# One decoder step: the keys' rotation in larger operations, a transpose without its copy, a split made one block ahead, and a new order in layer 1

## The chip, the cores and the metric

The kernel runs on one core of a Trainium2 chip. The metric is device time in microseconds of one execution; lower is better. The engines go by short names: PE (TensorE, matmuls and transposes; PEld is its weight load), DVE (VectorE), ACT (ScalarE), POOL (GpSimd), SP (SyncE, which issues most DMAs).

## The reference, cut to what matters

One step of a two-layer decoder on 512 prompt tokens and 8 x 4 sample tokens (544 columns), model width 1024. Layer 0 mixes tokens with a gated linear recurrence (HGRN2), layer 1 with sparse attention: an indexer scores all keys, the best are kept, and softmax attention runs over those. In both layers the tokens also attend to 256 memory tokens, and each layer ends with a gated channel mixer. What the change touches in layer 1:

```python
def dsa_project(z, pos, q_norm, k_norm, ik_norm):
    q, k, v, iq, ik, iw = jnp.split(z, np.cumsum(DSA_SIZES)[:-1].tolist(), axis=-1)
    q = rope(rms_norm(q.reshape(B, T, N_Q_HEADS, HEAD_DIM), q_norm), pos)      # 6 heads of 128
    k = rope(rms_norm(k.reshape(B, T, N_KV_HEADS, HEAD_DIM), k_norm), pos)     # 2 heads of 128
    iq = rope(iq.reshape(B, T, IDX_HEADS, IDX_DIM), pos)                       # 8 heads of 64
    ik = rope(rms_norm(ik, ik_norm)[:, :, None, :], pos)[:, :, 0, :]           # 1 head of 64
def rope(x, pos):     # x1, x2: the halves of the last axis
    return jnp.concatenate([x1 * cos - x2 * sin, x2 * cos + x1 * sin], axis=-1)
def memory_keys_values(mem, w_kv, k_norm):
    k, v = jnp.split(mem @ w_kv, 2, axis=-1)
    return rms_norm(k.reshape(B, M, MEM_HEADS, MEM_HD), k_norm), v.reshape(B, M, MEM_HEADS, MEM_HD)
def memory_attention(zq, q_norm, mk, mv):
    q = rms_norm(zq.reshape(B, T, MEM_HEADS, MEM_HD), q_norm)
    s = jnp.einsum('bthd,bmhd->bhtm', q, mk) * (MEM_HD ** -0.5)
```

## The kernel before

All products are of fp32 quality: both factors are split into a high part and a low rest, and three matmuls, high x high, high x low and low x high, are summed in PSUM. The weights come as 199 units of 128 x 1024 in the order in which they are used (class `Weights`). Each is loaded (`raw`), copied by ACT to `whi`, and DVE or POOL subtracts to get `wlo`; in layer 1 POOL does it in four pieces of 256 columns (`W.piece`), and the loads are issued from POOL's queue (`W.queue`). Activations are split into `hi` and `lo` in the same way (`split`).

Every engine works through its own list in order; the lists are fixed when the program is built. The main program walks through the projections (`proj_fm` for outputs with features on the partitions, 48 matmuls of 272 columns for one unit of weights; `proj_tm` for outputs with tokens on the partitions). All else (norms, rotations, the indexer, the choice of keys, attention) is written as Python generators that issue a few instructions and yield. Between the groups of matmuls the main program calls `pump.run`, and there the string `SCRIPT` says which generators take a step: each letter or sign names a generator in the order of their making, a number repeats, a dot ends the call. A "+" or "-" in it answers a question: is this unit's `wlo` made by DVE (+) or POOL (-), is a row scaling (`scale_rows`) done by ACT (+) or DVE (-). So `SCRIPT` alone sets what stands ahead of what on each engine.

Layer 1 runs in this order: index keys and queries (`ikT`: transposes of the rotated index keys `ikr`; `id`: scores of the prompt's queries, which use `ikm`, a masked copy of `ikT`), v, the six query heads q with the first memory loads in between, k, attention, memory queries (mq) and memory keys and values (mkv). Beside the query heads run the steps of `choose_sample`, which searches the threshold of the best keys of the sample tokens by counting: each step is a few short DVE operations, three counts on DVE and four on ACT, and a small matmul (`ple_choose_sample` in the trace) that joins the counts. `choose_prompt` does the same for prompt tokens with MAX8 and MATCH_REPLACE8 on DVE; these have time and act as fillers. `query_scale` computes the norm factors of all query heads (`qss`, `rq`, `rqs`) and transposes those of the sample tokens (`qrb`).

`key_rope` rotates keys for index keys (5 tiles of 128 tokens, 1 head of 64) and for keys (2 + 2 + 1 tiles, 2 heads of 128): POOL multiplies by the cosine (into `ikr` or `kr`), DVE the swapped halves by the sine (`t_index_keys`, `t_keys`), then DVE subtracts and adds. `mem_kv` projects the memory: four blocks of `raw` memory columns, each split into high and low and then multiplied with one weight unit (matmul `mkv` of 512 columns). `mem_samples` computes the norm factors of the sample tokens' memory queries (`m_mem_samples`, `mrs`), spreads four of them over 64 columns each with a POOL copy (`rqx`), and transposes that into PSUM (`mb`) to scale the queries (`mqz`).

## Time and profile before

| | us |
|---|---|
| median of 3 timed runs | 1492.82 (1492.29 to 1493.84) |
| the profiled execution's own time | 1481.36 |
| its span in the trace | 1479.6 |
| mean granted clock of PE | 0.982 of 2.4 GHz |
| PE busy | 1428.4 |
| DVE, ACT, POOL busy | 797.0, 587.3, 578.5 |

The profiled execution was one of its own, beside the timed runs; its time is the span and 1.8 us around it. All durations below are from it. "Busy" counts an engine's instructions without its waits.

### The profile page before, as it was taken

Reading aid. Unit: us, or ns where it says so; the run is one execution under the profiler, and the core shown is the slowest. Engines: PE = TensorE matmul, PEld = TensorE weight load, DVE = VectorE, ACT = ScalarE, POOL = GpSimd, SP = SyncE. Lnnn points to the kernel's source line nnn. Section 1 sums busy time; section 2 is a strip of 40 time slices with the busy share of each in tenths; the row PEclk is TensorE's granted clock in tenths of the full one; section 3 lists DMA queues with packets and bytes.
Section 4 is the critical chain, followed back from the end, with each engine's and each line's share of the span. In section 5 each row is a group of like instructions: output and inputs, shape, how many; then the busy total and the mean of one; then the engine's idle time right before and its main releaser. Section 6 shows DMA issues by size and latency. Waiting matters only on the chain.

```text
span 1479.6 us, 28277 instructions
## 1 busy us (share of the span) xinstructions
PE 1428.4 (97%) x11314; PEld 1341.1 (91%) x11314; DVE 797.0 (54%) x1762; ACT 587.3 (40%) x1064; POOL 578.5 (39%) x663
## 2 busy tenths in 40 slices
PE   7989999999999999999999987799999999999998
PEld 7968889999999999999987876466999999999998
DVE  7366877754444224444378879876544442344431
ACT  5447465533333113333326452575333331233320
POOL 4332354423444024446764554460134441144410
PEclk9999999999999999999999997999999999999999
DMA  7341223222322322334322425750223333222331
GB/s 246 129 141 62 75 91 102 89 86 77 99 88 86 100 72 86 91 92 125 123 89 66 152 94 172 238 177 28 86 77 92 93 89 88 82 86 87 92 117 58
DMA packets 58995, 152.54 MB, mean 103 GB/s; under 512 B 7888, under 2 KB 21808, under 8 KB 58864
## 3 DMA queue, kind: packets, MB, share of 16 engines
q1 hardware_dynamic: 49792, 122.84, 27.0%
q0 software_dynamic: 8208, 26.50, 5.4%
q8 instruction: 89, 1.46, 0.4%
q10 hardware_dynamic: 864, 1.40, 0.3%
q14 instruction: 42, 0.34, 0.1%
HBM read 142.23 MB, written 8.47 MB: 102 GB/s over the span
## 4 chain that ended last, share of the span: by engine, by line
PE 84%; DVE 7%; issue 3%; POOL 2%; ACT 2%; DMA 1%; SPq 0%; ACTq 0%; POOLq 0%; DVEq 0%
PE a L420 73%; PE u_hgrn_head L420 1%; POOL wlo L420 1%; PE id_index_prompt L420 1%; PE ho_hgrn_head L420 1%; PE ms_prompt L420 1%; PE hgrn_head_samples L420 1%; PE as_prompt_attn L420 1%; DVE lo L420 1%; PE mkv L420 1%; PE mo_prompt L420 1%; PE sc_hgrn_head L420 1%; DMA raw<-w 1%; PE ao_prompt_attn L420 1%; PE mpt_prompt L420 1%
## 5 line engine op out<-in xcount | busy, mean ns | idle before, releaser
L420 POOL TENSOR_TENSOR wlo<-raw,whi 128x1024 fp32r<-128x1024 f32 (+1 forms) x206 | 353.9, 1729 | 560.1 <-ACT whi L420 536.0
L420 PE MATMUL a<-hi,whi 128*128 128x272 f32 x2640 | 554.6, 291 | 0.8 <-DVE ext L420 0.5
L420 PE MATMUL a<-lo,whi 128*128 128x272 f32 x2640 | 548.9, 289 | 5.6 <-DVE lo L420 5.6
L420 PE MATMUL a<-hi,wlo 128*128 128x272 f32 x2640 | 548.0, 289 | 0.0
L420 PEld LDWEIGHTS a<-hi,whi 128*128 128x128 f32 x2640 | 416.0, 189 | 8.5 <-issue 5.6
L420 PEld LDWEIGHTS a<-lo,whi 128*128 128x128 f32 x2640 | 416.2, 189 | 7.0 <-DVE lo L420 7.0
L420 PEld LDWEIGHTS a<-hi,wlo 128*128 128x128 f32 x2640 | 416.7, 189 | 0.0
L420 ACT ACTIVATE whi<-raw 128x1024 fp32r<-128x1024 f32 (+1 forms) x202 | 209.5, 1038 | 243.9 <-PE a L420 153.6
L420 DVE TENSOR_TENSOR wlo<-raw,whi 128x1024 fp32r<-128x1024 f32 (+1 forms) x59 | 79.4, 1345 | 161.4 <-ACT whi L420 161.2
L420 DVE TENSOR_TENSOR sc<-a,rb 128x544 f32<-128x544 f32 x53 | 38.4, 725 | 114.9 <-PE a L420 113.3
L420 DVE SCALAR_TENSOR_TENSOR conv<-ext,params,conv 128x560 f32<-128x560 f32 x88 | 70.6, 802 | 47.7 <-ACT conv L420 46.2
L420 DVE TENSOR_TENSOR ext<-a,rb 128x240 f32<-128x240 f32 x132 | 37.6, 340 | 105.8 <-PE a L420 98.3
L420 ACT ACTIVATE conv<-ext,params 128x560 f32<-128x560 f32 x44 | 37.7, 856 | 135.0 <-DVE ext L420 114.1
L420 ACT ACTIVATE hi<-sc 128x544 fp32r<-128x544 f32 x44 | 29.0, 659 | 137.5 <-DVE sc L420 137.5
L420 DVE TENSOR_TENSOR x<-a,x 128x544 f32<-128x544 f32 x48 | 34.7, 723 | 78.9 <-PE a L420 78.5
L420 POOL TENSOR_TENSOR sqa<-sqa,sq 128x544 f32<-128x544 f32 x24 | 34.7, 1447 | 107.4 <-ACT sq L420 107.1
L420 DVE TENSOR_TENSOR sc<-sc,conv 128x512 f32<-128x512 f32 x88 | 65.8, 786 | 4.6
L420 ACT ACTIVATE conv<-conv 128x560 f32<-128x560 f32 x44 | 29.6, 672 | 73.8 <-DVE conv L420 73.8
L420 ACT ACTIVATE hi<-x,params 128x544 fp32r<-128x544 f32 x32 | 23.8, 745 | 68.9 <-DVE x L420 68.9
L420 DVE TENSOR_TENSOR lo<-sc,hi 128x544 fp32r<-128x544 f32 x44 | 31.9, 725 | 31.9 <-ACT hi L420 31.9
L420 PE MATMUL a<-whi,hi 128*128 128x256 f32 x160 | 47.0, 294 | 0.0
L420 PE MATMUL a<-whi,lo 128*128 128x256 f32 x160 | 45.1, 282 | 0.0
(406 smaller groups left out, 1918.0 us busy)
## 6 DMA issues: line engine op xcount, KB each, us to landing
raw<-w SPq DMA_DIRECT2D x177, 512.0 KB, 3.5
raw<-w POOLq DMA_DIRECT2D x21, 512.0 KB, 4.1
k_sample_scores<-ckT SPq DMA_DIRECT2D x46, 128.0 KB, 2.1
ck_mem_samples<-cmkT SPq DMA_DIRECT2D x16, 256.0 KB, 5.5
cv_mem_samples<-cmv SPq DMA_DIRECT2D x16, 256.0 KB, 5.6
st_s<-hgrn_head_samples POOLq DMA_DIRECT2D x12, 256.0 KB, 3.0
hgrn_head_samples<-hst SPq DMA_DIRECT2D x10, 256.0 KB, 3.8
ck_sample_scores<-ckT SPq DMA_DIRECT2D x18, 128.0 KB, 2.3
```

The lines of the kernel that those rows point to most:

```text
L420: return f(*args, **kw)
```

## The change

Four edits. `key_rope` takes its cosine and sine from views over all tiles of a key tensor (`qtab`, `itab` are now one view for each tensor), and so multiplies a whole tensor's half at once: for the index keys 2 operations of 128x160 on each of POOL and DVE instead of 10 of 128x32, for the keys 6 on each instead of 10. `mem_samples` leaves out the copy `rqx`: four matmuls with the identity take the broadcast factor itself as the other operand (32 x 64), each giving 64 of the 128 rows of `mb`. `mem_kv` splits block u + 1 before the matmuls of block u. And the part of `SCRIPT` that plays layer 1 is another one, of the same number of calls.

```diff
-    "12.+12.+17.-e6.e2.-2.e8.-5.-2f2.f5.f3.-.f9.-4.f.f9.-gh6.3g.16g2i12gi2gi4gj4gi8gh2g4hjij2h.-ijihjl.lij.i.ji.j.ij."
+    "12.+12.+17.-e6.e2.-2.e8.-5.-2f2.f3.f5.+3.f7.+4.f7.f.2g.h.+4.g.g.2g.26gi2g2hi4gigj2i7gighghjig2hjijg.-ghihjilij4."
...
@@ mem_kv
+        pump.run(raw[0])
+        x = split(raw[0][:, :512], sl=slice(0, 512), eng=G if POOLED else V)
         for u in range(4):
+            xh, xl = x
             if len(raw) < min(u + 3, 4):
                 mem_load(raw)
-            pump.run(raw[u])
-            xh, xl = split(raw[u][:, :512], sl=slice(0, 512), eng=G if POOLED else V)
             hi, lo = W.next()
+            if u < 3:
+                pump.run(raw[u + 1])
+                x = split(raw[u + 1][:, :512], sl=slice(0, 512), eng=G if POOLED else V)
@@ mem_samples
-        rx = slot(name="rqx")
-        G.tensor_copy(v3(rx[0:NS, :256], 4, 64), v3(rq[0:NS], 5, 4)[:, 4, :].unsqueeze(2).to_broadcast([NS, 4, 64]))
-
-        yield [rx]
+
+        yield [rq]
         bb = bank("mb")
         for j in range(2):
-            T.transpose(bb[:, 32 * j:32 * j + 32], rx[0:NS, 128 * j:128 * j + 128], ident[0:NS, 0:NS])
+            for e in range(2):
+                T.matmul(bb[64 * e:64 * e + 64, 32 * j:32 * j + 32],
+                         rq[0:NS, 16 + 2 * j + e:17 + 2 * j + e].to_broadcast([NS, 64]), ident[0:NS, 0:NS],
+                         start=True, stop=True, skip_group_check=True)
@@ key_rope
-            for i in range(n):
-                c4 = tabs[at][:, 0:hf].unsqueeze(1).to_broadcast([128, nh, hf])
-                s4 = tabs[at][:, hf:].unsqueeze(1).to_broadcast([128, nh, hf])
-                for sl, other in ((slice(0, hf), slice(hf, d)), (slice(hf, d), slice(0, hf))):
-                    G.tensor_mul(f(t1)[:, i, :, sl], k4[:, i, :, sl], c4)
-                    V.tensor_mul(f(t2)[:, i, :, sl], k4[:, i, :, other], s4)
-                at += 1
+            cs, sn = (tab[:, :, sl].unsqueeze(2).to_broadcast([128, n, nh, hf]) for sl in (slice(0, hf), slice(hf, d)))
+            for sl, other in ((slice(0, hf), slice(hf, d)), (slice(hf, d), slice(0, hf))):
+                G.tensor_mul(f(t1)[:, :, :, sl], k4[:, :, :, sl], cs)
+                V.tensor_mul(f(t2)[:, :, :, sl], k4[:, :, :, other], sn)
@@ layer 1
-    qtab = [tt[j // 4][:, 128 * (j % 4):128 * (j % 4) + 128] for j in range(5)]
-    itab = [tt[1][:, 128 + 64 * j:192 + 64 * j] for j in range(5)]
+    qtab = [v3(tt[0][:, 0:256], 2, 128), v3(tt[0][:, 256:512], 2, 128), v3(tt[1][:, 0:128], 1, 128)]
+    itab = [v3(tt[1][:, 128:448], 5, 64)]
```

In layer 0 the order of the instructions stays as it was but for the two edited functions. In layer 1 the new `SCRIPT` gives seven more weight units' `wlo` to DVE: two of the v projection, one of the first query head, two of the k projection and two of the output projection (59 before, 66 now); five row scalings go from DVE to ACT. Among its moves: choice step 2 of the sample tokens stands behind 42 of the 48 matmuls of the first query head, where it stood behind 12 of the next one. Three places of the new order follow; names carry a number that only tells tiles apart.

DVE at the index keys' rotation, before (`rq`, `t_2`, `t_3`: the rotation of index queries):

```order
L420 TENSOR_TENSOR ikt_index_keys_2_8490<-ikt_index_keys_2_8490,params_79 128x320
L420 TENSOR_TENSOR rq_8564<-a_8483,tab_8305 128x544
L420 TENSOR_TENSOR t_2_8565<-a_8483,tab_8307 64x544 x2
L420 TENSOR_TENSOR t_index_keys_1_8584<-ikt_index_keys_2_8490,tt_8293 128x32 x10
L420 TENSOR_TENSOR rq_8647<-a_8577,tab_8305 128x544
L420 TENSOR_TENSOR t_3_8648<-a_8577,tab_8307 64x544 x2
L420 TENSOR_TENSOR ikr_8463<-ikr_8463,t_index_keys_1_8584 128x5x32 x2
L420 TENSOR_TENSOR wm_8302<-wm_index_keys_1_8707,consts_81 128x32
```

The same place now:

```order
L420 TENSOR_TENSOR ikt_index_keys_2_8490<-ikt_index_keys_2_8490,params_79 128x320
L420 TENSOR_TENSOR rq_8564<-a_8483,tab_8305 128x544
L420 TENSOR_TENSOR t_2_8565<-a_8483,tab_8307 64x544 x2
L420 TENSOR_TENSOR wlo_8571<-raw_8316,whi_8570 128x1024
L420 TENSOR_TENSOR t_index_keys_1_8593<-ikt_index_keys_2_8490,tt_8293 128x5x32 x2
L420 TENSOR_TENSOR rq_8628<-a_8574,tab_8305 128x544
L420 TENSOR_TENSOR t_3_8629<-a_8574,tab_8307 64x544 x2
L420 TENSOR_TENSOR wlo_8635<-raw_8399,whi_8634 128x1024
L420 TENSOR_TENSOR ikr_8463<-ikr_8463,t_index_keys_1_8593 128x5x32 x2
```

The products `t_index` are now two, and a weight split stands ahead of them and another ahead of `ikr`.

PE at the transposes of the rotated index keys, before, where 18 matmuls of the last index query projection (`a_8660`) and then the v projection (`a_8780`) stand behind them:

```order
L420 MATMUL ikT_index_keys_2_8696<-consts_80,ikr_8463 64x32
L420 MATMUL wm_index_keys_1_8707<-sc_8459,consts_81 128x32
L420 MATMUL a_8660<-hi_8110,whi_8474 128x272 x2
L420 MATMUL a_8660<-lo_8111,whi_8474 128x272 x2
L420 MATMUL a_8660<-hi_8110,wlo_8475 128x272 x2
L420 MATMUL a_8660<-hi_8196,whi_8474 128x272 x2
L420 MATMUL a_8660<-lo_8197,whi_8474 128x272 x2
L420 MATMUL a_8660<-hi_8196,wlo_8475 128x272 x2
L420 MATMUL a_8660<-hi_8282,whi_8474 128x272 x2
L420 MATMUL a_8660<-lo_8283,whi_8474 128x272 x2
L420 MATMUL a_8660<-hi_8282,wlo_8475 128x272 x2
L420 MATMUL a_8780<-whi_8570,hi_7670 128x256
```

The same place now:

```order
L420 MATMUL a_8638<-lo_8283,whi_8474 128x272 x2
L420 MATMUL a_8638<-hi_8282,wlo_8475 128x272 x2
L420 MATMUL ikT_index_keys_1_8698<-consts_80,ikr_8463 64x128 x4
L420 MATMUL ikT_index_keys_2_8699<-consts_80,ikr_8463 64x32
L420 MATMUL wm_index_keys_1_8710<-sc_8459,consts_81 128x32
L420 MATMUL id_index_prompt_1_8747<-ikm_8464,rq_8468 128x256
L420 MATMUL a_8762<-whi_8570,hi_7670 128x256
```

The projection (`a_8638`) is now complete ahead of `ikT`, and the first scores `id` follow `wm` at once.

DVE at the query scale, before, where MATCH_REPLACE and MAX of `choose_prompt` stand between the copy of `qss` and its chain:

```order
L420 COPY qss<-qst_query_squares_1_9970 128x5x3
L420 MATCH_REPLACE isc_index_prompt_2_8889<-_prompt_choose_prompt_2_8940,isc_index_prompt_2_8889 128x384
L420 MATCH_REPLACE isc_index_prompt_1_8843<-_prompt_choose_prompt_2_8886,isc_index_prompt_1_8843 128x256
L420 MAX _prompt_choose_prompt_1_8939<-isc_index_prompt_2_8889 128x8
L420 TENSOR_TENSOR qss<-qss,rs_8290 128x30 x2
L420 TENSOR_SCALAR qss<-qss 128x30
L420 TENSOR_SCALAR m_query_scale_1_10013<-qss 128x30
```

The same place now:

```order
L420 COPY qss<-qst_query_squares_1_9924 128x5x3
L420 TENSOR_SCALAR _sample_choose_sample_2_9021<-_sample_choose_sample_9_9931,_sample_choose_sample_2_9021 128x7
L420 TENSOR_SCALAR _sample_choose_sample_1_9020<-_sample_choose_sample_2_9021 128x1
L420 TENSOR_TENSOR _sample_choose_sample_1_9020<-_sample_choose_sample_1_9020 128x7
L420 TENSOR_TENSOR _sample_choose_sample_1_9020<-_sample_choose_sample_1_9020 128x1
L420 TENSOR_TENSOR _sample_choose_sample_1_9020<-consts_81,_sample_choose_sample_1_9020 128x7
L420 TENSOR_SCALAR _sample_choose_sample_1_9025,_sample_choose_sample_4_9023<-row_index_sample_3_9015,_sample_choose_sample_1_9020,_sample_choose_sample_2_9021 128x264 x3
L420 TENSOR_TENSOR qss<-qss,rs_8290 128x30 x2
L420 TENSOR_SCALAR qss<-qss 128x30
L420 TENSOR_SCALAR m_query_scale_1_9979<-qss 128x30
```

The choice step of the sample tokens that stood ahead of the copy now stands behind it, and the chain follows without `choose_prompt`'s operations.

DVE at the memory block, before; eight operations on `sbias` follow, then the additions `kr`, the memory norm factors and the second `lo`:

```order
L420 COPY m_mem_samples_1_10439<-mst_mem_samples_1_10440 128x5x2
L420 TENSOR_TENSOR t_keys_1_10447<-v_10060,tt_8292 128x2x64 x4
L420 TENSOR_TENSOR t_keys_2_10448<-v_10063,tt_8292 128x2x64 x4
L420 TENSOR_TENSOR t_keys_3_10449<-v_last_1_10085,tt_8293 128x2x64 x2
L420 TENSOR_TENSOR lo_10492<-mem_8769,hi_10491 128x512
L420 COPY m_mem_samples_1_10439<-mst_mem_samples_2_10504 128x5x2
L420 COPY _sample_choose_sample_2_9044<-ample_choose_sample_13_10544 128x2
L420 SCALAR_TENSOR_TENSOR _sample_choose_sample_1_9048<-consts_80,_sample_choose_sample_2_9044,row_index_sample_3_9039 128x256
L420 SCALAR_TENSOR_TENSOR _sample_choose_sample_1_9048<-consts_80,_sample_choose_sample_2_9044,row_index_sample_3_9039 128x8
L420 SCALAR_TENSOR_TENSOR _sample_choose_sample_1_9048<-_sample_choose_sample_1_9048,row_index_sample_3_9039 128x264
L420 SCALAR_TENSOR_TENSOR _sample_choose_sample_1_9048<-row_index_sample_3_9039,_sample_choose_sample_2_9044,_sample_choose_sample_1_9048 128x264
```

The same place now:

```order
L420 TENSOR_TENSOR t_keys_1_10442<-v_10027,tt_8292 128x4x64 x2
L420 TENSOR_TENSOR t_keys_2_10443<-v_10030,tt_8292 128x4x64 x2
L420 TENSOR_TENSOR t_keys_3_10444<-v_last_1_10052,tt_8293 128x2x64 x2
L420 COPY m_mem_samples_1_10465<-mst_mem_samples_1_10467 128x5x2
L420 TENSOR_TENSOR kr_10046<-kr_10046,t_keys_1_10442 128x4x64 x2
L420 TENSOR_TENSOR kr_10047<-kr_10047,t_keys_2_10443 128x4x64 x2
L420 TENSOR_TENSOR kr_10048<-kr_10048,t_keys_3_10444 128x2x64 x2
L420 COPY m_mem_samples_1_10465<-mst_mem_samples_2_10480 128x5x2
L420 TENSOR_TENSOR lo_10489<-mem_8751,hi_10466 128x512
L420 MATCH_REPLACE isc_index_prompt_1_8812<-_prompt_choose_prompt_1_8891,isc_index_prompt_1_8812 128x256
L420 TENSOR_TENSOR m_mem_samples_1_10465<-m_mem_samples_1_10465,rs_8290 128x20 x2
```

The additions `kr` and the first `lo` now come directly behind `t_keys`, and the memory norm factors behind them.

On PE the transposes `kT` of `kr`, which stood behind the first 12 matmuls `mkv` and 8 sample scores, now stand ahead of these.

## Rows read from the trace of the kernel before

**Rows 1.** Part 1 of the page: busy time of each engine, its share of the span, and its instructions.
```profile
PE 1428.4 (97%) x11314; PEld 1341.1 (91%) x11314; DVE 797.0 (54%) x1762; ACT 587.3 (40%) x1064; POOL 578.5 (39%) x663
```

**Rows 2.** Busy time by stretches, layer 0 with the start of layer 1, and the channel mixer of layer 1. Columns: stretch in us, its length, busy us (and instructions) of each engine, granted clock of PE as a share of 2.4 GHz, busy share of the DMA engines, GB/s.
```profile
0.00:750.00 750.00, 735.86 (x5932) 703.83 (x5933) 394.21 (x799) 307.20 (x512) 307.42 (x318) 0.99 0.33 104
...
1029.00:1479.60 450.60, 446.63 (x3561) 446.01 (x3559) 172.32 (x268) 130.65 (x158) 139.48 (x145) 1.00 0.28 86
```

**Rows 3.** The same view for the rest of layer 1 (first row) and, inside it, for seven stretches of 3.4 to 10.2 us.
```profile
750.00:1029.00 279.00, 245.95 (x1825) 191.31 (x1823) 230.47 (x697) 149.43 (x394) 131.60 (x201) 0.93 0.40 128
774.90:778.30 3.40, 3.40 (x18) 3.40 (x17) 0.00 (x0) 3.25 (x11) 1.11 (x2) 0.50 0.25 82
829.50:832.90 3.40, 3.40 (x17) 3.40 (x16) 3.25 (x9) 0.70 (x3) 2.19 (x3) 0.50 0.82 274
877.30:884.10 6.80, 5.74 (x34) 4.24 (x34) 4.56 (x26) 4.15 (x13) 2.25 (x5) 0.50 0.78 260
901.20:911.40 10.20, 5.87 (x21) 4.25 (x15) 9.95 (x35) 0.90 (x2) 4.90 (x9) 0.50 0.47 142
918.30:925.10 6.80, 5.31 (x15) 3.67 (x19) 4.75 (x18) 0.50 (x1) 2.02 (x5) 0.50 0.84 247
945.60:949.00 3.40, 3.40 (x28) 1.50 (x30) 2.90 (x14) 0.76 (x3) 0.00 (x0) 0.50 0.74 247
959.20:962.60 3.40, 3.40 (x19) 1.42 (x20) 2.26 (x10) 1.36 (x5) 2.49 (x4) 0.51 0.74 239
```

**Rows 4.** PE's timeline at its waits in layer 1. Columns: start, busy us, engine, line, operation, out<-in, shape, count; in brackets the idle time before and who ended it.
```profile
773.41 0.77 PE L420 MATMUL ikT_index_keys<-consts,ikr 128*64 128x128 f32 x5 [3.41 <-DVE ikr L420]
...
827.75 0.61 PE L420 MATMUL ple_choose_sample<-ple_choose_sample,consts 128*128 128x4 f32 x4 [1.96 <-ACT ple_choose_sample L420]
...
828.55 0.41 PE L420 MATMUL a<-lo,whi 128*128 128x272 f32 x2
828.80 0.41 PE L420 MATMUL a<-hi,wlo 128*128 128x272 f32 x2
...
852.80 0.38 PE L420 MATMUL ple_choose_sample<-ple_choose_sample,consts 128*128 128x4 f32 x2 [1.03 <-ACT ple_choose_sample L420]
...
859.87 0.50 PE L420 MATMUL ple_choose_sample<-ple_choose_sample,consts 128*128 128x4 f32 x3 [1.08 <-ACT ple_choose_sample L420]
...
878.36 0.71 PE L420 MATMUL qrb_query_scale<-consts,rq 32*128 32x32 f32 x5 [2.95 <-DVE rq L420]
...
907.52 0.80 PE L420 MATMUL mkv<-whi,lo 128*128 128x512 f32 x1 [3.18 <-DVE lo L420]
...
916.50 0.31 PE L420 MATMUL mb_mem_samples<-consts,rqx_mem_samples 32*128 32x32 f32 x2 [2.10 <-POOL rqx_mem_samples L420]
...
919.79 0.80 PE L420 MATMUL mkv<-whi,lo 128*128 128x512 f32 x1 [1.89 <-DVE lo L420]
...
945.31 0.47 PE L420 MATMUL apt_prompt_attn<-consts,p_prompt_attn 128*128 128x128 f32 x2 [3.47 <-DVE p_prompt_attn L420]
```

**Rows 5.** The index keys' rotation: two rows of DVE's timeline, one of ACT's, and the page's group of weight splits made on DVE (busy us, mean ns of one).
```profile
762.27 0.49 DVE L420 TENSOR_TENSOR ikt_index_keys<-ikt_index_keys,params 128x320 f32<-128x320 f32 x1
...
764.90 4.63 DVE L420 TENSOR_TENSOR t_index_keys<-ikt_index_keys,tt 128x32 f32<-128x32 f32 x10
...
774.08 2.40 ACT L420 ACTIVATE ikm<-ikT_index_keys 32x512 f32<-32x512 f32 x4 [6.94 <-PE ikT_index_keys L420]
...
L420 DVE TENSOR_TENSOR wlo<-raw,whi 128x1024 fp32r<-128x1024 f32 (+1 forms) x59 | 79.4, 1345 | 161.4 <-ACT whi L420 161.2
```

**Rows 6.** The query scale: DVE's timeline, and POOL's at the same time.
```profile
871.68 0.08 DVE L420 MATCH_VALUE_LOAD isc_index_prompt<-mpt_choose_prompt,isc_index_prompt 128x8 f32 x1
...
872.60 0.55 DVE L420 MAX8 mpt_choose_prompt<-isc_index_prompt 128x8 f32<-128x384 f32 x1
...
874.82 0.67 DVE L420 TENSOR_TENSOR m_query_scale<-rq 128x30 f32<-128x30 f32 x1
...
877.58 0.19 DVE L420 TENSOR_TENSOR m_query_scale<-m_query_scale,qss 128x30 f32<-128x30 f32 x1
...
874.72 2.77 POOL L420 TENSOR_TENSOR wlo<-raw,whi 128x256 fp32r<-128x256 f32 x4 [5.14 <-ACT whi L420]
```

**Rows 7.** The memory block: DVE's timeline, and POOL's.
```profile
902.64 3.82 DVE L420 TENSOR_TENSOR t_keys<-v,tt 128x128 f32<-128x128 f32 x8
...
906.79 0.68 DVE L420 TENSOR_TENSOR lo<-mem,hi 128x512 fp32r<-128x512 f32 x1
...
911.07 1.83 DVE L420 TENSOR_TENSOR kr<-kr,t_keys 128x256 f32<-128x256 f32 x6
...
916.10 3.63 DVE L420 TENSOR_TENSOR lo<-mem,hi 128x512 fp32r<-128x512 f32 x1
...
897.25 4.54 POOL L420 TENSOR_TENSOR kr<-v,tt 128x128 f32<-128x128 f32 x8 [2.34 <-DVE v L420]
...
916.05 0.39 POOL L420 COPY rqx_mem_samples<-m_mem_samples 32x256 f32<-32x256 f32 x1 [9.66 <-DVE m_mem_samples L420]
916.42 2.77 POOL L420 TENSOR_TENSOR wlo<-raw,whi 128x256 fp32r<-128x256 f32 x4
```

**Rows 8.** The first scaling of attention weights of the second block of tokens, DVE's timeline.
```profile
941.35 0.69 DVE L420 MAX8 pt_choose_prompt<-isc_index_prompt 128x8 f32<-128x512 f32 x1
...
944.90 0.35 DVE L420 TENSOR_SCALAR p_prompt_attn<-p_prompt_attn,m_prompt_attn 128x256 f32<-128x256 f32 x1
```

## What the change should do to the time

> **What bounds the kernel now.** I read four views, from the whole to the single wait. First the busy times of the page: TensorE (PE) works 97% of the span [rows 1], so the kernel is bound by PE, and only two things can shorten it: time in which PE stands still, or time in which it runs at half its rate. Second the stretches: before 750 us and after 1029 us PE is busy 735.86 of 750 and 446.63 of 450.6 us at a granted clock of 0.99 and 1.00 [rows 2]. Nothing there is worth more than the change's small edits. Between them, in layer 1 from the index keys to the end of attention, PE is busy 245.95 of 279.00 us, so it stands still for 33.05 us, while VectorE (DVE) is busy 230.47 us, 83% [rows 3]. That stretch holds everything to be won, and DVE is the engine that sets its waits. Third the clock: seven stretches inside it, 37.4 us together, have a granted clock of 0.50 or 0.51 instead of about 1, so 1.2 instead of 2.4 GHz [rows 3]. PE is busy 30.52 us in them; at full rate that work would take half, so at most 15.3 us lie there. Fourth PE's own timeline: which instruction waited, how long, and for whom [rows 4]. The long waits are 3.41 us (transposes ikT of the rotated index keys, for DVE), 1.96 (a choice step of the sample tokens), 2.95 (qrb, the query scale, for DVE), 3.18, 2.10 and 1.89 (memory keys: for DVE's lo, POOL's rqx, DVE's lo) and 3.47 us (first transposes of the attention weights, for DVE). A half-clock stretch begins 1 to 2 us behind most of them: 773.41 and 774.90, 827.75 and 829.50. The waits of 1.03 and 1.08 us have none behind them [rows 3, 4]. A long wait removed can therefore pay twice.
>
> **T1, index keys: +3.8 us.** Ten DVE multiplications t_index of 128x32 took 4.63 us, 0.46 each, beside ten equal ones on POOL [rows 5]. Now there are two of 128x160 on each. A DVE product of 128x320 took 0.49 us [rows 5], so 128x160 alone is about 0.33 and two are 0.7: the lower bound. If DVE must take turns with POOL's two, at about 0.5 each (a POOL piece of 128x256 took 2.77/4 = 0.69 [rows 6]), four in turn are 1.7: the upper bound, which I take, since the rows of 0.46 look like turns. That saves 2.9 us of DVE. But the new order puts two whole weight splits (wlo, 1.345 us each [rows 5]) on DVE ahead of the end of ikr, 2.7 us. So DVE ends about where it did, and what shortens the wait is that PE now does the remaining 18 projection matmuls first (0.125 us each, by two starts 0.25 us apart for a pair [rows 4]): 2.3 us. Wait 3.41 - 2.9 + 2.7 - 2.3 = 0.9; with half of the 0.9 taken off because one split should fall into the time DVE waited for whi copies, 0.4: gain 3.0. The half-clock stretch behind it held 3.40 us of busy PE, half of which comes back: +1.7. The index products id now follow at once, and need two of the four copies ikm (2.40 us for four [rows 5]) that projection matmuls hid: 1.2 us less wm, -0.9. Bounds: 5.1 (no new wait) to -0.6 (each split also waits for an addition on POOL, the clock drop stays).
>
> **T2, query heads and choice steps: -1.5 us.** Choice step 2 moves from 12 matmuls into the first query head to 42 into the projection before it, 18 matmuls or 2.3 us earlier, behind fillers (top-k steps) on DVE. The wait of 1.96 us at step 3 and its clock drop (3.40/2 = 1.7) go; step 2 now waits about 2.1 and gets the drop. Steps 7 and 8, which waited 1.03 and 1.08 [rows 4], each get a DVE split of 1.345 in front of them, of which about 1 comes back because POOL no longer makes that split beside the step's small operations: 1.4 each. Steps 4 to 6 get some 1.4 in all where they had under one. 1.96 + 1.7 + 2.1 gone, 2.1 + 1.7 + 2.8 + 0.7 come: -1.5. Bounds -4 (all splits in full) to +3.7 (step 2 doesn't wait).
>
> **T3, query scale: +4.1 us.** Two fillers stood between the copy of qss and its chain, 871.68 to 873.15 us: 1.4 us [rows 6]; they now come after. Of the chain's short operations four took 0.65 to 0.67 us instead of 0.19 while POOL made pieces of wlo [rows 6]: 4 x 0.47 = 1.9 us, which stays if POOL's split still falls there. Wait 2.95 becomes between 1.55 and 0; I take 0.9. Of the 5.74 us of busy PE in the half-clock stretch [rows 3] up to 2.87 return; I take 2.05. Bounds 1.4 to 5.8.
>
> The Trainium skill (SBUF — State Buffer, Who interferes with whom) says that a DVE instruction with two SBUF inputs and a GpSimd one that reads SBUF exclude each other, and that whoever issues first keeps the shared ports for its whole instruction. The trace agrees: 0.65 is one POOL piece of 0.69, and the split lo that took 0.68 alone took 3.63 under a POOL split of 2.77 [rows 6, 7]. By the rule every DVE split also locks POOL for its 1.345 us, which is the slower rival below. Without that lock the sum is the 13.8 below; with every split held for one more POOL operation of its length, 9.4 us, it is 4.4.
>
> **T4, memory block: +4.6 us.** Today PE waits 3.18 for the first lo (DVE did t_keys, 3.82 us, before it), 2.10 for rqx, 1.89 for the second lo [rows 4, 7]: 7.17. In the new order the transposes kT stand ahead of the first memory matmuls and need the additions kr (1.83 us [rows 7]). DVE begins t_keys at 902.64 as before; in four larger pieces and two small ones it takes 2.1 (alone) to 2.9 (turns with POOL), so kr is ready at 906.6 to 907.4, and PE, there at 904.3 (907.52 - 3.18), waits 2.2 to 3.1: I take 3.0. What is late next: lo follows at once and its 0.68 lies beside the eight transposes. The copy rqx on POOL is gone, and the memory scale (912.83 to 916.1 today, 3.3 us of chain) now starts at about 908.5 and ends by 912, before PE has done 12 memory matmuls and 8 scores. The second lo follows it without a POOL split ahead of it. So 7.17 - 3.0 = 4.2, and 0.4 of clock, since a 3 us wait still precedes the same matmuls. Bounds 0 (the wait at kT is as long as all three) to 7.6 (2.2, and half of 5.31 us of the stretch 918.3 to 925.1 [rows 3]).
>
> **T5, attention: +2.8 us.** Eight fillers ran from 941.35 to 944.71 while PE waited 3.47 us for the first scaled weights at 944.90 [rows 4, 8]. Fewer now stand there: wait about 1.1, gain 2.4, and of the 1.7 us of clock I take 1.0. Two splits of the out projection go to DVE, 2.7 us; their POOL pieces cease, so net -0.6. Bounds -2 to +6.
>
> **At nothing:** the edits in layer 0 (same order; PE 98% busy; bounds -1 to +1), two more transposes of K=32 (four products instead of two, 0.16 us each by the wait row of 0.31 for two [rows 4]), and five row scalings on ACT instead of DVE (ACT is busy 149 of 279 us [rows 3]; without that cover 0.35 us each, as the row of 944.90 [rows 8]).
>
> **Sum:** 3.8 - 1.5 + 4.1 + 4.6 + 2.8 = 13.8 us. The profiled execution took 1481.36 us: 1467.6. The median of the timed runs is 1492.82, 11.46 us above the profiled one; I take this as an offset of the measurement that stays, so the forecast is 1492.82 - 13.8 = 1479.0.
>
> **Rivals.** (a) The clock returns wholly: if no wait in the stretch is long enough to be followed by half rate, up to 15.3 us come back instead of the 3.4 + 1.7 that T1, T3, T4 and T5 count net of T2, some 8 to 10 more: about 1470. For it speaks that T1 and T3 nearly empty their waits; against it the wait that T4 makes before kT and T2's new one. (b) The stalls only move: DVE, at 83%, works through the same list in another order, and every wait removed comes up at the next PE instruction that needs it. The change takes about 3 + 2 us of small operations from DVE and adds 7 splits, 9.4 us, so its load rises from 230 to about 235 of 279 us; gain 0 +- 3: 1493. For it speaks this load; against it that three of the removed waits are on an order, not on load (fillers ahead of an urgent chain). (c) Slower: DVE becomes the bound. The seven added splits are 7 x 1.345 = 9.4 us; if each of them also waits for one POOL addition of the rotated queries or piece (about 1.35 us, as the 3.63 us lo did), 18.9 us are on PE's path and the 13.8 are gone: +5.1, 1498. It decides when more than 13.8 of these 18.9 us reach PE, so from nearly all of the splits with half of their waits. Against it: most of them stand while DVE has idle time behind whi.
>
> **How the numbers follow.** Chances: the forecast with its own range of 3 to 20 us gained (1473 to 1490) 0.62; (a) 0.14; (b) 0.14; (c) 0.10. The bounds of the terms add up to -6 and +28, but they are independent, so the likely part is about 8 to either side. The range 1467 to 1493 takes in (a) and the faster half of (b), and leaves out (c), the slower half of (b) and a little below: under 0.2. A difference of 0.2%, 3 us, is about what a measurement tells from none. Faster: forecast and (a), 0.76; same: (b), 0.14; slower: (c), 0.10.
>
> **What would show it.** T1: ikT waits under 1 us, no half clock near 775 us, and a wait of about 1 us before the first id. T2: a wait of about 2 us at choice step 2, about 1.4 at 7 and 8. T3: the qss chain follows the choice step, qrb waits under 1.6. T4: one wait of 2 to 3 us before kT, none at the memory matmuls or mb. T5: first apt of the second token block waits about 1. The forecast is wrong if DVE's splits run far over 1.345 us, if PE's idle time between 750 and 1029 us stays near 33, or if waits of equal length turn up at id, choice 2 and kT, each followed by half clock.

## The result, and the profile after

The changed kernel took 1514.78 us (median of 4 runs, 1513.03 to 1515.3) where the kernel before took 1492.55 beside it: ratio 1.0129, interval 1.0105 to 1.0153. It is 22 us slower; 13.8 us faster were forecast, and the range did not hold it. PE's line of the page, against [rows 1]:

```profile
PE 1445.5 (96%) x11326; PEld 1352.6 (89%) x11326; DVE 795.5 (53%) x1752; ACT 591.9 (39%) x1069; POOL 560.8 (37%) x621
```

PE does 12 instructions more and is busy 17 us longer than in the first trace of the kernel before, 5 us longer than in a second one (1440.2): part of the loss is clock (the rate of 2.4 or 1.2 GHz that PE is granted), not idle time. To see where, I cut layer 1 at the same instructions in both kernels: norm of the index keys (`ikt`), first choice step, `qrb`, first `kT` or `mkv`, second `mss`, `mot`. For the kernel before I use a second trace of it (run e1; span 1499.3), since its first trace turned out to be a special case, as told below. The view of stretches, the changed kernel first:

```profile
core 0: us, PE busy (x) PEld busy (x) DVE busy (x) ACT busy (x) POOL busy (x), PEclk, DMA share, GB/s
755.93:809.27 53.34, 51.54 (x382) 41.13 (x381) 44.47 (x92) 26.68 (x61) 22.76 (x42) 1.00 0.19 60
809.27:882.83 73.56, 63.48 (x475) 58.77 (x471) 59.56 (x186) 36.65 (x97) 33.90 (x48) 0.91 0.31 100
882.83:911.60 28.77, 24.34 (x187) 21.80 (x187) 25.00 (x84) 11.43 (x24) 13.25 (x20) 0.85 0.53 169
911.60:952.62 41.02, 33.42 (x209) 22.70 (x209) 33.53 (x122) 19.32 (x52) 7.96 (x13) 0.82 0.74 233
952.62:1057.53 104.91, 78.90 (x519) 47.84 (x519) 60.34 (x196) 55.90 (x157) 33.52 (x34) 0.84 0.31 101
```

The same five stretches of the kernel before, second trace:

```profile
755.58:812.60 57.02, 53.32 (x382) 42.98 (x380) 45.71 (x99) 26.97 (x61) 30.48 (x62) 0.97 0.15 45
812.60:881.22 68.62, 60.09 (x475) 55.87 (x471) 59.78 (x186) 35.62 (x95) 35.98 (x53) 0.98 0.38 116
881.22:906.36 25.14, 23.71 (x187) 20.58 (x187) 18.96 (x71) 12.60 (x27) 14.41 (x26) 0.86 0.62 195
906.36:950.69 44.33, 32.36 (x199) 21.15 (x202) 39.09 (x141) 18.49 (x52) 14.60 (x24) 0.81 0.71 221
950.69:1045.35 94.66, 78.83 (x538) 50.20 (x532) 63.55 (x195) 54.03 (x154) 33.59 (x34) 0.86 0.33 108
```

The rows are the index keys, the query heads with the query scale, the memory queries, the keys' transposes with the memory block, and the attention. Row by row the change brings -3.7 us, +4.9, +3.6, -3.3 and +10.2, and behind `mot` 456.1 against 454.0, +2.1 (span less the last end). That is 14 of the 22; the two traces' spans differ by just that.

PE's waits in the changed kernel, in its timeline (start, duration, instruction, in brackets the wait and what ended it), to be held against [rows 4]:

```profile
775.39 0.77 PE L420 MATMUL ikT_index_keys<-consts,ikr 128*64 128x128 f32 x5 [0.80 <-DVE ikr L420]
777.35 0.70 PE L420 MATMUL id_index_prompt<-ikm,rq 128*128 128x256 f32 x2 [1.00 <-ACT ikm L420]
817.16 0.82 PE L420 MATMUL ple_choose_sample<-ple_choose_sample,consts 128*128 128x2 f32 x4 [1.70 <-ACT ple_choose_sample L420]
843.38 1.02 PE L420 MATMUL ple_choose_sample<-ple_choose_sample,consts 128*128 128x4 f32 x4 [4.76 <-ACT ple_choose_sample L420]
863.89 0.61 PE L420 MATMUL ple_choose_sample<-ple_choose_sample,consts 128*128 128x4 f32 x4 [1.52 <-ACT ple_choose_sample L420]
882.83 0.50 PE L420 MATMUL qrb_query_scale<-consts,rq 32*128 32x32 f32 x6 [1.77 <-DVE rq L420]
884.23 1.21 PE L420 MATMUL ss_sample_scores<-ck_sample_scores,qS 128*32 128x256 f32 x16
889.63 1.01 PE L420 MATMUL e_choose_sample<-ple_choose_sample,consts 128*128 128x4 f32 x4 [4.20 <-ACT ple_choose_sample L420]
913.12 1.60 PE L420 MATMUL kT_keys<-consts,kr 128*128 128x128 f32 x6 [0.85 <-DVE kr L420]
925.54 0.46 PE L420 MATMUL as_prompt_attn<-kT,rq 128*128 128x128 f32 x2 [1.97 <-DVE mqz_mem_samples L420]
927.68 1.28 PE L420 MATMUL as_prompt_attn<-kT,rq 128*128 128x128 f32 x4 [1.69 <-DVE m_prompt_attn L420]
949.68 0.44 PE L420 MATMUL apt_prompt_attn<-consts,p_prompt_attn 128*128 128x128 f32 x2 [0.91 <-DVE p_prompt_attn L420]
960.97 2.24 PE L420 MATMUL ss_sample_scores<-k_sample_scores,qS 128*32 128x256 f32 x16 [4.21 <-ACT ct_prompt_attn L420]
```

Three waits over 4 us are new up to here: choice step 5 at 843.38, choice step 11 at 889.63 (`e_choose_sample`; PE's work between steps 10 and 11 is the 16 short score matmuls at 884.23), and the sample scores at 960.97, which waited 1.94 in the kernel before:

```profile
953.76 0.60 PE L420 MATMUL ss_sample_scores<-k_sample_scores,qS 128*32 128x256 f32 x3 [1.94 <-ACT ct_prompt_attn L420]
```

What stood ahead of step 5 on DVE and POOL, and the same pair of DVE operations some steps earlier:

```profile
836.88 3.89 DVE L420 TENSOR_TENSOR ple_choose_sample<-ple_choose_sample 128x7 int32<-128x7 int32 x2
836.59 1.37 POOL L420 TENSOR_TENSOR rq<-rq,t 128x544 f32<-128x544 f32 x1
837.90 2.77 POOL L420 TENSOR_TENSOR wlo<-raw,whi 128x256 fp32r<-128x256 f32 x4
820.67 0.24 DVE L420 TENSOR_TENSOR ple_choose_sample<-ple_choose_sample 128x7 int32<-128x7 int32 x2 [0.47 <-DVE ple_choose_sample L420]
```

A pair of operations on seven numbers for each partition takes 3.89 us and ends as POOL's rotation addition and weight split end. At the other steps of this kernel it takes 0.24 to 0.94, in the kernel before 0.23 to 1.05.

### The profile page after: what moved, and what is told of

The parts are those of the page before. It is cut to its first block, busy times and chain, and to the rows that moved or that the text cites. A ratio compares the mean times of both kernels' runs of the same rounds, so it can differ in the third digit from the quotient of the medians.

```text
span 1513.6 us, 28254 instructions
## 1 busy us (share of the span) xinstructions
PE 1445.5 (96%) x11326; PEld 1352.6 (89%) x11326; DVE 795.5 (53%) x1752; ACT 591.9 (39%) x1069; POOL 560.8 (37%) x621
## 5 line engine op out<-in xcount | busy, mean ns | idle before, releaser
L420 POOL TENSOR_TENSOR wlo<-raw,whi 128x1024 fp32r<-128x1024 f32 (+1 forms) x178 | 335.1, 1891 | 575.1 <-ACT whi L420 555.1
L420 DVE TENSOR_TENSOR wlo<-raw,whi 128x1024 fp32r<-128x1024 f32 (+1 forms) x66 | 88.4, 1339 | 167.8 <-ACT whi L420 161.3
```

The source lines that it names most:

```text
L420: return f(*args, **kw)
```

## The experiments

`SCRIPT` makes 2061 calls in either kernel. Call 1157 begins the first query head, 1266 stands behind the k projection, 1297 behind the memory queries (the expectations of e5 and e10 name these two points one projection too early), 1319 behind the memory projection; nearly all of the attention is played in 1320. A mixed order takes its calls from one kernel up to such a point and from the other behind it; steps still due are made up there. The mixed orders that play calls 1298 to 1318 as before differ from it in three answers on who makes a row scaling (calls 1308 and 1311). Each group of runs stood on one chip, with runs of the kernel before on it. The two columns of times are medians in us; the ratio, with its 95% interval, is taken over the runs and is not the quotient of the medians (1.0100 for e2, whose four runs spread from 1509 to 1522):

| run | what is new | before beside it | this | ratio (interval) |
|---|---|---|---|---|
| e1 | nothing | 1498.12 | 1501.09 (one) | |
| e2 | order | 1498.12 | 1513.06 | 1.0135 (1.0086 to 1.0185) |
| e3 | edits | 1498.12 | 1497.52 | 1.0000 (0.9972 to 1.0027) |
| e4 | all, splits on POOL | 1498.12 | 1515.11 | 1.0127 (1.0087 to 1.0167) |
| e5 | edits, order to 1265 | 1496.39 | 1498.06 | 1.0010 (0.9999 to 1.0021) |
| e6 | edits, order to 1318 | 1496.39 | 1503.82 | 1.0055 (1.0038 to 1.0072) |
| e7 | edits, order from 1319 | 1496.39 | 1503.44 | 1.0053 (1.0036 to 1.0070) |
| e8 | edits, order to 1156 | 1479.72 | 1480.10 | 1.0004 (0.9993 to 1.0016) |
| e9 | e7, sample path early | 1479.72 | 1490.11 | 1.0068 (1.0051 to 1.0086) |
| e10 | edits, order to 1296 | 1479.72 | 1487.09 | 1.0052 (1.0034 to 1.0071) |
| e11 | e10, step 2 back | 1479.09 | 1482.61 | 1.0023 (1.0009 to 1.0037) |
| e12 | e10, step 11 back | 1479.09 | 1483.26 | 1.0031 (1.0018 to 1.0045) |
| e13 | edits, first part of attention | 1479.09 | 1474.96 | 0.9973 (0.9959 to 0.9987) |
| e14 | edits, second part of attention | 1479.09 | 1486.42 | 1.0045 (1.0029 to 1.0061) |
| e15 | all, again | 1496.75 | 1519.21 | 1.0152 (1.0133 to 1.0171) |
| e16 | e8 and e13 | 1496.75 | 1506.36 | 1.0053 (1.0032 to 1.0073) |
| e17 | e11, e12 and e13 | 1496.75 | 1505.60 | 1.0048 (1.0028 to 1.0067) |
| e18 | no gathers, else before | 1480.60 | 1481.42 | 1.0001 (0.9986 to 1.0017) |

**Order or edits (e1 to e3).** e1 has no edit; e2 and e3 swap one part:

```diff
 e2, in the kernel before
-SCRIPT of before
+SCRIPT of after
 e3, in the kernel after
-SCRIPT of after
+SCRIPT of before
```

> The kernel before, unchanged, for a second trace on the chip of these runs. The trace on which the prediction rests took 1481.4 us, the timed runs 1491 to 1494. Theory 1 (a disturbance that both kernels meet, and that trace by chance did not): this trace takes about 1492, and its 11 us more stand in single stretches in which PE, DVE and ACT stand still together, as the trace of the changed kernel shows near 967 to 972 us. Theory 2 (those stretches belong to the changed kernel): none of them here, and the time is about 1481 or the 11 us are spread over everything.

> The kernel before with the new order alone (the new SCRIPT, the seven splits on DVE and five row scalings on ACT with it); rotation, rqx and the memory split as before. Order theory (the moves cost the time): about +22 us or more against the kernel before, 1510 to 1520. Edit theory (the larger operations, the four small products or the split ahead cost it): within 5 us of the kernel before.

> The three edits alone, played by the old SCRIPT, all splits where they were. Order theory: as fast as the kernel before or faster, -2 to -10 us, since the wait of 3.4 us for ikr shrinks by the 2.9 us of smaller rotation work and the rqx wait of 2.1 us goes. Edit theory: slower by 15 us or more.

As far as the intervals tell, the whole loss is in the order; the three edits by themselves are worth nothing that can be told, 4 us either way (e3). e1 shows that the first trace was a quick one by 20 us, nearly all of it in the attention, second `mss` to `mot`: 77.31 us there, 94.66 in the row above.

```profile
948.27:1025.58 77.31, 69.42 (x538) 44.43 (x531) 63.35 (x195) 53.40 (x154) 33.63 (x34) 0.97 0.39 125
```

**The splits (e4), rival (c).**

```diff
-                if pump.pick(model.t["dve"] <= late):
+                if pump.pick(model.t["dve"] <= late) and u not in (112, 113, 114, 120, 121, 128, 129):
```

> The changed kernel with the seven weight splits of layer 1 back on POOL (v, first query head, k, out projection), all else in its new order. Split theory (DVE carries 9.4 us too much and locks POOL): 10 us or more of the 22 come back, 1495 to 1505. Order theory (the moves themselves): within 5 us of the changed kernel, 1510 to 1520.

With the seven splits back on POOL nothing changes, and choice step 5 waits as long:

```profile
841.24 1.01 PE L420 MATMUL ple_choose_sample<-ple_choose_sample,consts 128*128 128x4 f32 x4 [5.10 <-ACT ple_choose_sample L420]
834.74 3.89 DVE L420 TENSOR_TENSOR ple_choose_sample<-ple_choose_sample 128x7 int32<-128x7 int32 x2
```

So the splits neither cause the loss nor this wait.

**Which calls (e5 to e10).**

```diff
-calls 0 to 2060 of after
+e5: 0 to 1265 of after, from 1266 of before
+e6: 0 to 1318 of after, from 1319 of before
+e7: 0 to 1318 of before, from 1319 of after
+e8: 0 to 1156 of after, from 1157 of before
+e10: 0 to 1296 of after, from 1297 of before
 e9, in call 1320 of e7: the same steps, these moved forward
+sample_values 2, 3 behind prompt_attn6 11
+sample_attn 2 to 8 from behind prompt_attn1 16 on
```

> The changed kernel, but its new order ends with the v projection and the query heads (index keys, choice steps, query scale); from the k projection on the old order stands, with the old choice of engines for splits and scalings. Early theory (the cost lies in the index, choice and query scale moves): still 12 us or more slower than the kernel before. Late theory (it lies behind them): between 2 us slower and 6 us faster than the kernel before, since the ikT wait and its half-clock stretch are gone.

> The changed kernel with the new order up to the end of the memory matmuls, and the old order for what follows: the rest of attention, the sample tokens' values and memory attention. Attention theory (the cost lies in that rest, where the trace of the changed kernel falls back 12 of its 14 us against the second trace of before): within 5 us of the kernel before. Memory-block theory (the moves at k, memory and first attention block cost it): 10 us or more slower.

> The opposite: the old order up to the end of the memory matmuls, the new order from there on. Attention theory: 10 to 17 us slower than the kernel before. Memory-block theory: within 5 us of it.

> The changed code, with the new order only up to the end of the index part (through the index scores, the v projection and step 1 of the sample tokens' choice) and the old order from there on. Theory: the early part of the new order is right by itself (in the trace of the changed kernel the stretch from the index keys' norm to the first choice step is 3.7 us shorter than in the second trace of the kernel before), and the new order up to the k projection comes out 1.7 us slower only because its choice steps among the query heads cost 6.5 us. Then this kernel is 2 to 4 us faster than before: ratio 0.9975 +- 0.001, and the choice steps show waits as before. Rival: what the index part gains is lost at the next wait, whatever order follows; ratio 1.000, with PE's idle time between the first choice step and the query scale larger than before by 3 us.

> Old order to the end of the memory projection and new order from there, as in the run that cost 7.1 us, but with the sample tokens' own path moved forward to where the old order has it: the issue of the gathers of the chosen values and the first seven steps of the sample tokens' attention stand ahead of the weight transposes of the second token block's last head. Theory: the 7.1 us come from this path, which reaches its matmuls 6 to 17 us later in the new order; then the ratio falls from 1.005 to between 1.000 and 1.002. Rival: they come from the prompt tokens' attention, whose six token blocks are interleaved step by step in the new order, so that each short product waits for ACT or DVE and the clock stays at half; then the ratio stays at 1.004 to 1.006, and the half-clock time between the second mss and the third mo_prompt at some 40 us.

> The changed code, new order to the end of the k projection and the query scale, old order from the transposes of the rotated keys on. Theory: the 5.7 us that the new order costs between the k projection and the end of the memory projection come from its first half (the choice steps among the k projection, behind which PE waits up to 4.2 us); then this kernel is slower than before by 5 to 7 us, ratio 1.0035 to 1.005. Rival: they come from the memory block itself and the attention steps played beside it (keys' transposes ahead of the first memory products, token blocks interleaved); then it stays at +1.7 us, ratio 1.000 to 1.002.

e5 costs 1.7 us: its trace holds the whole loss of the choice steps (64.85 us for steps 1 to 9), nearly made up at the index keys and the query scale. e6 and e7 cost 7.4 and 7.1 us, so neither of their theories held: the loss lies about half ahead of call 1319 and half behind it. The two add up to 14.5 us, where the whole cost 22 on other chips; what makes the rest was not found.

The index part alone gains nothing in all (e8), as the rival had it, but not where the rival had it: the stretch from the first choice step to `qrb` took 66.04 us, 1.9 less than in the first trace of the kernel before, and the gain is lost from `qrb` to the second `mss` (72.60 against 69.91). e10 costs 7.4 us, as much as e6 on another chip; so, as far as two chips can be compared, the early loss is made before call 1297, and the memory block behind it adds none and gains none. In e9 the sample path, forecast as the cause, is early, and the loss of the attention stays (10 us): that theory fell.

**Two single steps (e11, e12), in e10's order, on PE.**

```diff
 e11: choice step 2
-behind 42 matmuls of the first query head
+behind 12 matmuls of the second query head
 e12: choice step 11
-behind 16 ss_sample_scores, ahead of the memory queries
+behind 24 matmuls of the memory queries
```

> The kernel with the new order to the end of the k projection (7.4 us slower than before), with one step moved back: choice step 2 of the sample tokens stands behind 12 matmuls of the second query head again, not behind 42 of the first. Theory: asked for early, its operations on VectorE push the first rotation of the queries behind them, so that two rotations run next to each other, GpSimd gets two additions and two weight splits in a row, and choice step 5 waits 4.8 us behind a VectorE product that cannot run beside them. Then with step 2 back, the stretch from choice step 1 to 9 falls from 64.3 to 57.5 - 59 us, step 5 waits under 1.5 us, and the ratio falls from 1.005 to 1.0005 +- 0.001. Rival: the weight splits that stand on VectorE at other places do it; then step 5 still waits 4 to 5 us and the ratio stays at 1.004 to 1.006.

> The same kernel (new order to the end of the k projection, 7.4 us slower than before), with one other step moved back: the joining matmuls of choice step 11 stand behind 24 projection matmuls again, not right behind the sample scores that follow step 10. Theory: PE's wait of 3.9 to 4.2 us at this place is only the order: step 11 needs VectorE's and ACT's counts, some 5 us, and nothing but 16 short score matmuls hides them. Then with the step back the wait is under 1 us, the half-clock stretch behind it shrinks, the stretch from the query scale to the first keys' transposes falls from 28.6 to 24 - 25.5 us, and the ratio from 1.005 to about 1.002 to 1.003. Rival: ACT's copy of the weights, which waits for its load ahead of ACT's counts, makes the step late in any case; then the wait only moves and the stretch stays over 27 us.

e10 ran on another chip than e11 and e12. e11 took the ratio from 1.0052 to 1.0023; steps 1 to 5 fell from 33.65 to 31.40 us, but steps 5 to 9 stayed at 30.3 (26.3 before). Step 5 now waits 1.79 (5.09 in e10), and the pair ahead of it on DVE takes 1.05 instead of 3.89:

```profile
839.29 0.61 PE L420 MATMUL ple_choose_sample<-ple_choose_sample,consts 128*128 128x4 f32 x4 [1.79 <-ACT ple_choose_sample L420]
835.63 1.05 DVE L420 TENSOR_TENSOR ple_choose_sample<-ple_choose_sample 128x7 int32<-128x7 int32 x2
```

So the early step 2 did it here: its operations stand ahead of the first rotation on DVE, two rotations then follow each other, and POOL gets two additions and splits in a row. That is 2.7 of the some 6 us that steps 1 to 9 lose, less than the theory had it (a stretch of 57.5 to 59 us; it took 61.67); step 8 keeps its wait of about 1.6. e12 took 1.0052 to 1.0031, within the noise of both (the intervals overlap), and step 11 waits 0.96 instead of about 4:

```profile
887.44 0.61 PE L420 MATMUL e_choose_sample<-ple_choose_sample,consts 128*128 128x4 f32 x4 [0.96 <-ACT ple_choose_sample L420]
```

The stretch from `qrb` to `kT` fell by only 1.0 us (28.56 to 27.53), as the rival had it: a later choice step then waits 1.79 and `kT` 2.63 instead of 0.80. Up to the second `mss` the traces show 3.7 us less (71.38 to 67.65).

**Two parts of the attention (e13, e14).** The cut is the end of the sample tokens' first weight transposes (`sample_attn` 8) in call 1320.

```diff
-calls 0 to 1318 of before, from 1319 of after
+e13: 0 to 1318 of before, 1319 and 1320 of after up to the cut, then of before
+e14: 0 to 1320 of before up to the cut, then of after
```

> Old order to the end of the memory projection, then the new order for the first part of the attention (up to the end of the sample tokens' first weight transposes), then the old order again. Theory: the 7 to 10 us of the new attention order are made in its second part, where token blocks 3 and 4, the memory products and the sample values are dealt out one step of each at a time; then this kernel is 0 to 3 us slower than before, ratio 1.000 to 1.002. Rival: the first part makes them, through the waits of the first weight transposes and the late sample scores: ratio 1.004 to 1.007.

> The other way round: old order to the end of the sample tokens' first weight transposes, new order from there. Theory: this kernel is 5 to 9 us slower than before, ratio 1.003 to 1.006, with some 20 us more at half clock than the old order has up to the third mo_prompt. Rival: 0 to 3 us slower, ratio 1.000 to 1.002. If both parts cost about half, the loss lies in the spread of the token blocks as such and in no one place.

On this chip e13 is 4.1 us faster than the kernel before and e14 7.3 us slower. So the second part makes the loss, as the theory had it; that e13 would be faster it had not (0 to 3 us slower). Both hold the three edits, and no run of the edits alone stood on this chip: of the 5.8 us by which e13's trace is shorter than the first one of the kernel before, 3.0 lie in the index keys' stretch (53.79 against 56.77), where only the edits are new. How much of the 4.1 us the first part brings is not shown. Second `mss` to `mot`, e13 first, then e14:

```profile
942.66:1020.15 77.49, 68.31 (x532) 44.30 (x532) 61.69 (x199) 56.59 (x162) 33.63 (x34) 0.96 0.40 125
948.13:1032.87 84.74, 73.52 (x526) 46.03 (x519) 59.13 (x187) 54.64 (x154) 33.57 (x34) 0.89 0.35 109
```

Of these 7.25 us only 2.0 are idle time (11.22 against 9.18). But e13's row holds a wait of 4.51 us at the sample scores `ss`, made by its first part, where e14 waits 1.60. From these scores to `mot`, in the same order:

```profile
950.68:1020.15 69.47, 65.18 (x505) 42.62 (x506) 54.28 (x173) 52.76 (x150) 30.54 (x32) 0.97 0.41 130
954.02:1032.87 78.85, 69.23 (x492) 43.37 (x493) 53.74 (x167) 51.00 (x145) 31.84 (x33) 0.89 0.37 115
```

Of 9.4 us 5.3 are idle time (9.62 against 4.29) and 4.1 are PE's own work at a lower granted clock, 0.89 instead of 0.97. What went ahead of the low clock, in e14:

```profile
963.00:968.00 5.00, 2.87 (x19) 2.21 (x19) 3.94 (x14) 4.87 (x12) 3.79 (x4) 1.00 0.67 216
968.00:973.00 5.00, 3.92 (x24) 2.46 (x23) 4.07 (x15) 3.64 (x11) 3.79 (x4) 1.00 0.67 212
973.00:978.00 5.00, 4.96 (x34) 2.39 (x34) 3.88 (x13) 3.00 (x7) 1.89 (x2) 0.63 0.54 179
978.00:983.00 5.00, 4.53 (x22) 3.13 (x15) 1.91 (x7) 2.21 (x4) 0.00 (x0) 0.50 0.01 3
```

No wait there is long (1.43 us at most). PE is thinly used for 10 us and then has full work at half rate, 0.50. Which step of the second part makes it thin was not tried.

**The whole and the sum (e15 to e17).**

```diff
 e15: the kernel after, unchanged
 e16, e17
-calls 0 to 2060 of after
+e16: 0 to 1156 of after, 1157 to 1318 of before, attention as in e13
+e17: 0 to 1296 of after with steps 2 and 11 back, to 1318 of before, attention as in e13
```

> The changed kernel itself, once more, beside the runs of the kernel before on the same chip. Theory: the loss is the sum of its places (choice steps 2 to 9 about 6, step 11 about 4, second part of attention about 7, against gains of 3.7 at the index keys and 4 in the first part of attention), so 8 to 12 us, ratio 1.005 to 1.008, if the chip shows no common idle stretches; on a chip that shows them, ratio 1.011 to 1.015, because they then come on top at other places. Rival: the parts interact, and the whole costs 20 us on any chip: ratio 1.012 to 1.015 without such stretches.

> New order up to choice step 1, old order to the end of the memory projection, new order in the first part of the attention, old order after it: the two stretches whose new order did not lose, put together. Theory: the gains add, 0 to 1 us from the first and 4.1 us from the second: 3.5 to 5 us faster than before, ratio 0.9965 to 0.9978. Rival: the first part of the attention gains only behind the old order of the early part, which it still has here from choice step 1 on; if it doesn't carry over, ratio 0.999 to 1.001.

> New order to the end of the k projection with both single steps moved back (choice steps 2 and 11), old order to the end of the memory projection, new in the first part of the attention, old after it. Theory: the single steps' gains add (ratio 1.005 less 0.003 less 0.002 gives about 1.000), and the first part of the attention gives 0.0027 more: ratio 0.997 to 0.9985. Rival: the two steps cure one and the same delay, then 1.000 to 1.0015.

This group fell on a chip of the slower kind (before 1496.75). The whole cost 22 us again, as both e15's theory and its rival have it on such a chip; on the quicker kind the changed kernel was not run. Its trace spreads the loss otherwise than the first trace of the same kernel. Choice steps 1 to 9 take 61.99 us instead of 64.80, with 2.72 at step 5 instead of 4.76; step 11 waits 5.64 instead of 4.20, and `kT` 3.27 instead of 0.85:

```profile
839.60 1.02 PE L420 MATMUL ple_choose_sample<-ple_choose_sample,consts 128*128 128x4 f32 x4 [2.72 <-ACT ple_choose_sample L420]
886.72 1.02 PE L420 MATMUL e_choose_sample<-ple_choose_sample,consts 128*128 128x4 f32 x4 [5.64 <-ACT ple_choose_sample L420]
910.18 2.18 PE L420 MATMUL kT_keys<-consts,kr 128*128 128x128 f32 x8 [3.27 <-DVE kr L420]
```

So the size of a single place, read from one trace, is good to some 2 to 3 us only.

e16 and e17, built from parts that gained or cost nothing on the other kind (e17's by adding up what e11 and e12 gave back), are 9 to 10 us slower, outside both theories. e16 plays the same order as e13 from the memory queries on, and takes 30 us more from second `mss` to `mot`, against 77.49 above:

```profile
942.83:1050.87 108.04, 82.22 (x532) 51.03 (x531) 61.71 (x199) 57.58 (x162) 33.58 (x34) 0.79 0.29 89
```

Where it begins, in e16 first, then in e13 on the quicker chip: the stretches in which the first gathers of the sample values are issued, and ACT's copies of the sample scores `sn`, whose last matmul ends at 953.5 in e16 and 953.35 in e13.

```profile
950.00:955.00 5.00, 3.35 (x50) 2.59 (x50) 3.57 (x13) 1.88 (x6) 3.92 (x5) 0.66 0.59 189
955.00:960.00 5.00, 0.91 (x2) 0.30 (x2) 0.00 (x0) 0.20 (x1) 3.78 (x5) 0.80 0.70 221
960.00:965.00 5.00, 1.76 (x7) 1.37 (x8) 1.21 (x5) 2.45 (x9) 0.82 (x1) 0.50 0.40 117
956.79 0.20 ACT L420 ACTIVATE sr<-sn_sample_scores 128x32 f32<-128x32 f32 x1 [3.27 <-remote]
962.55 0.20 ACT L420 ACTIVATE sr<-sn_sample_scores 128x32 f32<-128x32 f32 x1 [5.57 <-remote]
```

```profile
955.00:960.00 5.00, 4.92 (x42) 3.12 (x41) 4.42 (x20) 4.47 (x12) 3.78 (x5) 1.00 0.67 223
953.24 0.34 ACT L420 ACTIVATE sr<-sn_sample_scores 128x32 f32<-128x32 f32 x2
```

On the slower chip PE, DVE and ACT do next to nothing for 5 us (0.91, 0.00 and 0.20) while POOL issues gathers as on the other (3.78 in both), at nearly the same rate (221 and 223 GB/s). Then comes half clock.

**Are the gathers the cause (e18)?** In the kernel before:

```diff
-                gather(t[:, :512], a["cv"], vidx[:, n, 4 * g + b4:4 * g + b4 + 1])
+                at = 128 * (8 * n + 4 * g + b4)
+                G.dma_start(t[:, :512], a["cv"][at:at + 128])
```

> The kernel before with one thing changed: the 32 gathers of the sample tokens' chosen values (128 rows of 2 KB each, row numbers from a tile, issued by GpSimd) are plain loads of 128 neighbouring rows of the same size from the same queue, so the values that the sample tokens average are other rows than the chosen ones. All else stays in its order. Theory: on a chip that shows the common idle stretches the gathers cause them; then none is left behind 950 us, and the kernel is 10 to 18 us faster there, ratio 0.988 to 0.993. Rival: the stretches come from something else at that time (the stores of the memory keys and values, the loads beside them); then they stay, and the ratio is 0.998 to 1.001. On a chip without the stretches (before near 1479 us) both expect a ratio of 0.998 to 1.001, and the run tells nothing but that the gathers themselves cost nothing there.

It fell on a chip of the quicker kind (before 1480.60), where both expect nothing: ratio 1.0001. It tells only that the gathers cost nothing there.

## Why the prediction was wrong

**T1 was right:** `ikT` waits 0.80, `id` 1.00, the granted clock is 1.00 throughout, -3.7 us against -3.8. But the kernel with only this part new was not faster (e8; its stretch took 54.9 us, as in e10, and 53.3 to 53.4 in the other traces of this order). Of the 3.7, some 3.2 are the edits: with them and the old order the stretch took 53.8 us in four traces (e7, e9, e13, e14), 55.3 in e3. This fits the working, in which the splits and the matmuls put ahead nearly cancel; but the edits gain nothing by themselves either (e3).

**T2 (-1.5, bounds -4 to +3.7) failed in size:** choice steps 1 to 9 cost 6.5 us more (58.25 to 64.80), beyond the bound, and 3.7 more in e15, just inside it. The step of the working that failed is that step 3's wait of 1.96 us goes and "step 2 now waits about 2.1", with nothing more than splits behind it. Step 2 did wait 1.70; but I counted what it delays on PE and not what it pushes back on DVE and POOL, where two rotations came to stand together (e11). Steps 7 and 8 were forecast to wait 1.4 each behind a split on DVE; step 8 did (1.52), but not for the splits (e4).

The Trainium skill (SBUF — State Buffer, Who interferes with whom) says that VectorE instructions with two SBUF inputs and GpSimd's reads exclude each other. The trace agrees: 3.89 us for what takes 0.24 at 820.67, ending with POOL's 1.37 and 2.77. The prediction looked for this at the added splits; it struck the smallest operations of an urgent chain.

**T3 (+4.1) was right in kind, too large:** from step 9 to `qrb` 8.75 us instead of 10.37, +1.6, near the lower bound. `qrb` still waits 1.77, where 0.9 was taken.

**Left out: choice step 11.** No term spoke of it. The new order asks for it right behind step 10, and PE waits 4.20 (889.63). The memory queries' stretch, which I had at nothing, lost 3.6 us; e12 confirms the place by its wait of 0.96; the 3.1 us that its time gives back are within the noise.

**T4 (+4.6):** the wait at `kT` was 0.85, not 3.0 (3.27 in e15), and the three memory waits are gone, but `mqz` (1.97) and a factor of the attention, `m_prompt_attn` (1.69), are waited for instead. The stretch gained 3.3, but that includes the wait which T5 named. In e10, where `kT` stands ahead too and that wait (3.54) is still there, it took 42.82 us against 44.33 and 44.70 in the two traces of the kernel before: some 1.5 to 1.9, right in sign and less than half in size.

**T5 (+2.8, bounds -2 to +6) failed outright, and is the largest miss:** the attention lost 10.2 us, and 2.1 behind `mot`. I read one wait of it (3.47 at 945.31) and counted the rest as unchanged, though all its steps are dealt out anew. That wait did shrink, to 0.91 (949.68). But the sample scores right behind wait 4.21 instead of 1.94; they wait 3.9 to 5.5 in all traces whose first part of the attention is new, and under 3.6 in the others. And e14 shows the second part to cost 7.3 us, by short waits and by the clock, without a long wait. By the timed runs the attention made about half of the loss (7.1 us in e7), the calls ahead of it as much (7.4 in e6).

**The offset:** "11.46 us above the profiled one; I take this as an offset of the measurement that stays" was wrong. The trace came from a condition in which the attention takes 77 us; on chips on which the kernel before takes 1496 to 1498 us it takes 88 to 95 with the old order (e1, e3, e5, e6) and 100 to 110 with the new (the changed kernel, e2, e4, e7, e15) or its first part alone (e16, e17). The stretch in which the order matters most was read from the one trace that did not show its stalls.

**Rivals:** (a) no. (b), the stalls move, is what e8 and the sample scores show, but the price was 15 to 22 us, not 0. (c) is refuted by e4. None of the three had the attention as its place.

**What stays open:** step 8's wait; which step makes PE thin in the second part; why the two halves of the order cost 14.5 us on one chip and the whole 22 on others; and why the parts that cost nothing on one kind of chip cost 9 us on the other. The version that beat the kernel before (e13, 0.9973) was run on the quicker kind alone; the same attention lost on the other (e16), so it can't be called better.

## What to carry to other kernels

When an order is exchanged, list every wait that the new order can make, not only those that it removes: for each step that moves forward, ask what it now stands ahead of on each engine, and whether matmuls still lie between it and the step it waits for. A stretch whose steps are dealt out anew can't be priced from its one longest wait; look there at how thin PE's work gets: in e14 half rate followed such a stretch, with no wait over 1.43 us in the list. Take a second trace of the same kernel before pricing single places: here they moved by 2 to 3 us. And compare the profiled time with the timed ones before pricing: a gap of 0.8% was a stretch that looked otherwise in the runs that count.

## What the runs showed of the hardware that I had not expected

Two kinds of chips: the same kernel before took 1479 to 1481 us on three of them and 1496 to 1498 on three others (1492.55 beside the changed kernel's own runs). All traces of the second kind, old order or new, hold stretches in which PE, DVE and ACT stand together, 5 to 12 us in all (counting those of 0.3 us and more), beginning 2 to 6 us behind the first gathers, in all but e1's with ACT waiting for "remote" (3.27 and 5.57 us in e16; in the changed kernel's trace 2.57 and 6.23). With the new first part of the attention they are 5.3 to 11.8 us, with the old 4.7 to 6.4. The traces of the first kind, the first one of the kernel before among them, hold none. That the gathers cause them was argued from the place, and not shown.
